# An encoder trunk on one core: weight splits on VectorE below chunk 60, delta-net matmuls interleaved by head and direction, and a shorter inverse square root

## The chip, the cores and the metric

The kernel runs on one core of a Trainium2 chip. A core has five engines that run side by side, each through its own instruction stream in order: TensorE (PE; its weight loads are listed as PEld), VectorE (DVE), ScalarE (ACT), GpSimd (POOL) and SyncE (SP), which here issues nearly all DMAs. Matmuls write to PSUM, of which VectorE and ScalarE read the results; the other operands lie in SBUF. The metric is the device time of one execution in microseconds; less is better.

## The reference, cut to what matters

Two residual layers on 512 tokens of width 1024, in float32. The part that the change touches is the bidirectional gated delta net; the rest is summarised in comments.

```python
for l in range(DEPTH):                       # DEPTH = 2
    h = rms_norm(x, attn_norm[l])
    # one projection h @ w_in: neighbourhood attention (4 heads), sliding-window
    # attention (8 query heads, 2 key heads, rotary), delta net, three merge gates
    y_na = neighborhood_attention_2d(rms_norm(qa), rms_norm(ka), va, na_rpb[l])
    y_swa = sliding_window_gqa(apply_rope(rms_norm(qs)), apply_rope(rms_norm(ks_)), vs, sink)
    y_gdn = gated_deltanet_bidir(qkv_c, z_c, beta_c, a_c, ...)
    merged = (g_na * (y_na @ w_branch_na[l]) + g_swa * (y_swa @ w_branch_swa[l])
              + g_gdn * (y_gdn @ w_branch_gdn[l]))
    x = x + merged @ w_out[l]
    h = rms_norm(x, ffn_norm[l])
    u = depthwise_conv_centred(h @ w_up[l], ffn_conv_w[l]) + ffn_conv_b[l]
    a, b = jnp.split(u, 2, axis=-1)
    x = x + (jax.nn.silu(a) * b) @ w_down[l]

def gated_delta_rule_chunked(q, k, v, beta, g):      # 4 heads, 8 chunks of 64, both directions
    g = jnp.cumsum(g, axis=-1)
    decay = jnp.exp(jnp.where(incl, g[..., :, None] - g[..., None, :], -jnp.inf))
    k_beta = k * beta[..., None]
    lower = jnp.where(strict, einsum('bhnid,bhnjd->bhnij', k_beta, k) * decay, 0.0)
    # (lower + I) is inverted: u, w = its products with beta v and beta k exp(g)
    qk = einsum('bhnid,bhnjd->bhnij', q, k) * decay
    def step(S, xs):                                 # over the 8 chunks
        v_new = u_c - w_c @ S
        o_c = q_c @ S + qk_c @ v_new
        S = S * d_c + k_c.T @ v_new
        return S, o_c

def rms_norm(x, g):                                  # an inverse square root per token (and head)
    return x * lax.rsqrt(jnp.mean(x * x, axis=-1, keepdims=True) + NORM_EPS) * g
```

## The kernel before, in words

Features lie on the partitions and the 512 tokens along the free axis. Every weight matrix is cut into 128 chunks per layer (`wall`, chunk numbers `CH_...`): 0 to 59 belong to the projections, gates, branch projections and the output projection of the attention half, 60 to 103 (`CH_UP`) to the up-projection, 104 to 127 (`CH_DN`) to the down-projection. A chunk has 8 blocks of 128x128 and is read in two halves of four blocks.

Each product of a dense layer keeps float32 accuracy with three matmuls (`mm3`, L150 to L152): high weight x high input, high x low, low x high. `load_w` prepares a half chunk: SyncE reads `raw`, ScalarE rounds it to the high part `hi` (L142), and GpSimd computes the low part `lo = raw - hi` (L144). `raw`, `hi` and `lo` have three buffers each; a new `hi` waits until TensorE has used up the one three halves earlier.

`rsq` (L166 to L173) gives inverse square roots on VectorE, on 4 to 32 columns: one integer operation for the start value, then three Newton steps of three operations each, ten instructions that depend on one another. It is called ten times in a layer: by `Stream.finish` for each of the two norms of the layer, by `knorm` for the keys (three times), for the query norms of both attentions, for the keys of the delta net, and twice at its output. `spread` multiplies its result by the constant `RSQ`, and transposes it back to the layout of the features (L193); `sums` makes the sums of squares with narrow matmuls (L179), copies them to a tile `sb` and transposes them (L183).

The delta net goes through `gdn_gates`, `gdn_project`, `gdn_cross`, `gdn_solve`, `gdn_mid`, `gdn_scan` and `gdn_out`. Two heads share 128 partitions (64 each), and so do the two directions in the solve and the scan. In `gdn_cross` a loop over the four heads makes the decays (L662, L670), and per half of four chunks four matmuls (L677) of 64 contraction rows, which start at partition 0 or 64 as the head is even or odd; each head's eight matmuls stand one behind another. VectorE multiplies the results with the decays (L681, L682), and the triangular blocks are copied to `Xg` and `Xo` by GpSimd and ScalarE (L687, L692). `gdn_solve` transposes these and inverts 32x32 blocks by substitution: 31 steps of a product (L713) and a subtraction (L715) on VectorE, each on all heads and chunks; then matmuls join the blocks (L749, L764). In `gdn_mid`, L794 and L812 are 64x64 matmuls that alternate between the two directions, which lie in the two halves of the partitions and of the array. `gdn_scan` runs over eight steps; in each, L832 (`w x S`) and L843 (`k x v_new`) are eight 64x64 matmuls, first the four heads of one direction and then those of the other, and VectorE adds the results (L835, L848).

The order of work: the code issues the steps in the order `sp np gg na gp sa gx gz gs gm gc go mn ms mg` (projections and attentions, the delta net's steps `g.`, then the three merges), and the framework's planner (`TileContext(..., schedule_with_timeline_sim=True)`) lays down the order of each engine's stream ahead of the run, from priorities and assumed durations; dense matmuls of the gates fill in between the attention's matmuls. On the chip each engine keeps to its stream and waits where an input is not there.

Of the kernel before, what the change touches and what calls it, by code (L numbers as in the profile page):

```python
# [35 lines left out]
CH_UP = 60  # L36
# [7 lines left out]
ENG = {}  # L44
FIRST = {"np": CH_NA, "sp": CH_SK, "gp": CH_GK}
RSQ_K = 2.0 ** -65.5626
RSQ = -RSQ_K / 8
CAPS = {n + i: c for n, c in (("nqs", 2), ("nkh", 2), ("y", 4), ("ma", 4), ("mg", 8), ("gt", 2), ("W", 2),
                              ("qd", 2), ("wn", 2), ("vs", 1), ("z", 1), ("act", 22)) for i in "01"}
CAPS |= {"ysh": 2, "ysl": 2, "kE": 4, "kT": 4, "Q": 4, "VN": 4, "SA": 4, "kq": 4, "dup": 5, "spr": 4, "xo": 4, "qs0": 4, "qs1": 4, "kdh0": 1, "kdh1": 1, "kdl0": 1, "kdl1": 1, "nkl0": 2, "nkl1": 2, "sv": 1, "hf": 8}  # L50
# [11 lines left out]
def encoder_kernel(ctx, tc, xT, wall, par, cst, nab, out, depth=2, dbg=None):  # L62
# [70 lines left out]
    def load_w(l, c, nk=8):  # L133
        if (l, c) in early:
            return early.pop((l, c))
        ws = []
        for o in range(0, nk, 4):
            n = min(4, nk - o)
            raw = wp.tile([128, 4, 128], F32, tag="raw", name=nm("wr"), bufs=NB["raw"])
            lastw[0] = nc.sync.dma_start(out=raw[:, :n], in_=wall[l, c, :, o * 128:(o + n) * 128].rearrange("p (k m) -> p k m", k=n))  # L140
            hi = wp.tile([128, 4, 128], F32R, tag="hi", name=nm("wh"), bufs=NB["hi"])
            S.activation(out=hi[:, :n], in_=raw[:, :n], func=AF.Copy)  # L142
            lo = wp.tile([128, 4, 128], F32R, tag="lo", name=nm("wl"), bufs=NB["lo"])
            G.tensor_tensor(lo[:, :n], raw[:, :n], hi.bitcast(F32)[:, :n], op=ALU.subtract)  # L144
            ws += [(hi[:, k], lo[:, k]) for k in range(n)]
        return ws

# [15 lines left out]
        V.tensor_tensor(lo, src, hi.bitcast(F32), op=ALU.subtract)  # L163


    def rsq(a, n):  # L166
        y, t = small(n, "rq"), small(n, "rt", 1)
        V.tensor_scalar(y.bitcast(I32), a.bitcast(I32), 1, 0x7FFFFFFF, op0=ALU.logical_shift_right, op1=ALU.bitwise_xor)
        for i in range(3):
            V.scalar_tensor_tensor(t, y, RSQ_K / 2 ** i, a, op0=ALU.mult, op1=ALU.mult)  # L170
            V.scalar_tensor_tensor(t, t, RSQ_K / 2 ** i, y, op0=ALU.mult, op1=ALU.mult)
            V.scalar_tensor_tensor(y, t, -3.0, y, op0=ALU.add, op1=ALU.mult)  # L172
        return y  # L173


    def sums(src, sel, tag, pb=None):
        pb = bank(tag)[:, 0:256] if pb is None else pb
        for b in range(4):
            T.matmul(pb[32 * b:32 * b + 32, 0:128], lhsT=sel, rhs=src[:, 128 * b:128 * b + 128], start=True, stop=True,  # L179
                     tile_position=(0, 32 * b))  # L180
        sb = tmp(name="sb")[:, 0:128]
        copy("sb", sb, pb[:, 0:128])
        T.transpose(pb[:, 128:256], sb, ident)  # L183
        return pb[:, 128:256].rearrange("p (b i) -> p b i", b=4)[:, :, 0:32:16]
# [51 lines left out]
    def n8(a):  # L236
        return a.rearrange("p (n i) -> p n i", n=8)
# [37 lines left out]
    for l in range(depth):  # L275
# [374 lines left out]
        def gdn_cross():  # L650
            line[0] = "g"
            nonlocal Q, Qu, Xo, Xg, Lt, Rt, kds, qdec

            Q, Qu = by2("Q")
            Xo, Xg, Lt = (big(F32, (128, 32, 32), name=n) for n in ("Xo", "Xg", "Lt"))
            kds = [[doubled(kq[j][i][:, :, 0, :]) for i in range(2)] for j in range(2)]
            qdec = pair(name="qd") + pair(name="qd")
            for hh in range(4):
                j, rr = hh // 2, slice(64 * (hh % 2), 64 * (hh % 2) + 64)
                pe, pr = decay_sums(hh, (msr, blk))  # L660
                eg = tmp(name="eg")
                S.activation(out=eg, in_=pr, func=AF.Exp)  # L662
                for d in range(2):
                    r = slice(64 * d, 64 * d + 64)
                    for i in range(2):
                        ns = slice(4 * i, 4 * i + 4)
                        V.tensor_tensor(n8(qdec[hh])[r, ns], n8(eg)[r, ns], kq[j][i][rr, :, 1, :], op=ALU.mult)  # L667
                T.matmul(pe, lhsT=idb, rhs=nmb.unsqueeze(1).to_broadcast([128, 8, 64]), start=False, stop=True)
                e = tmp(name="E")
                S.activation(out=e, in_=pe, func=AF.Exp)  # L670
                on("ebk", "V").tensor_tensor(n8(e), n8(e), bc(bk, hh, 0, 8), op=ALU.mult)
                xt = tmp(name="X")
                for n0 in (0, 4):
                    kd = kds[j][n0 // 4]
                    pk = bank("gd")
                    for n in range(4):
                        T.matmul(pk[:, 128 * n:128 * n + 128], lhsT=kd[rr, n].rearrange("p d i -> p (d i)"),  # L677
                                 rhs=kq[j][n0 // 4][rr, n].rearrange("p c i -> p (c i)"), start=True, stop=True)
                    pkv = pk.rearrange("p (n c i) -> p c n i", n=4, c=2)
                    en = n8(e)[:, n0:n0 + 4]  # L680
                    V.tensor_tensor(n8(xt)[:, n0:n0 + 4], pkv[:, 0], en, op=ALU.mult)  # L681
                    V.tensor_tensor(Qu[n0 // 4 * 2 + hh // 2][:, :, hh % 2], pkv[:, 1], en, op=ALU.mult)  # L682

                for q4 in range(4):
                    r = slice(32 * q4, 32 * q4 + 32)
                    o = 32 * (q4 % 2)
                    cpx = (S.activation if q4 % 2 else G.tensor_copy)(  # L687
                        out=Xg[r].rearrange("p i (h n) -> p h n i", h=4)[:, hh], in_=n8(xt)[r, :, o:o + 32], **({"func": AF.Copy} if q4 % 2 else {}))
                    if q4 == 2:
                        lastg[0] = cpx  # L690
                    if q4 in (0, 3):
                        S.activation(out=Xo[r, 8 * hh:8 * hh + 8], in_=n8(xt)[r, :, 32 - o:64 - o], func=AF.Copy)  # L692
            Rt = big(F32, (128, 32, 32), "Rt")

        def gdn_solve():
# [121 lines left out]
        def gdn_scan():  # L817
# [7 lines left out]
            for s in range(8):  # L825
                ns = (s, 7 - s)
                half = [slice(0, 64), slice(64, 128)]
                if s:
                    pv = bank("gd", (128, 4, 64))
                    for d, r in enumerate(half):  # L830
                        for hh in range(4):
                            T.matmul(pv[r, hh], lhsT=n8(wn[hh])[r, ns[d]], rhs=SA(ns[d])[r, hh], start=True, stop=True,  # L832
                                     tile_position=(64 * d, 64 * d))
                    for d, r in enumerate(half):
                        V.tensor_tensor(VN(ns[d])[r], pv[r], VN(ns[d])[r], op=ALU.add)  # L835
                if s < 7:
# [295 lines left out]
```

## Time and profile before

| | us |
|---|---|
| median of 3 runs | 1711.9 |
| lowest and highest | 1708.8, 1712.89 |
| profiled execution, its own time | 1711.75 |
| its span in the trace, first to last instruction | 1710.0 |
| TensorE, VectorE, GpSimd, ScalarE busy | 1656.6, 1008.1, 834.5, 739.1 |

The profile is of one execution. A busy time counts an engine from the start of an instruction to its end; matmuls overlap, so a TensorE that is busy all the time need not be at its peak. In layer 0 the attention half ends at about 502 us and the MLP at about 866; layer 1 follows. The rows below have times in us from the start of the span, unless they are marked ns.

### The profile page before, as it was taken

The page shows a single profiled execution, that of the slowest core. Times are in us where ns is not written, and L with a number is a line of the kernel's source. Part 1 is how long each engine was busy: PE and PEld are TensorE (multiplying, and loading weights), DVE is VectorE, ACT ScalarE, POOL GpSimd, SP SyncE. Part 2 cuts the span into 40 slices and gives each one's busy share as a digit, 9 for nine tenths or more (in the row PEclk, how much of TensorE's full clock was granted, in tenths as well). Part 3 has the DMA queues.
Part 4 walks back from the last instruction along what each step waited for, and adds up shares of the span by engine and source line. Part 5 has one row for each costly group of instructions (what it writes and reads, how often), then busy time and mean ns, then how long its engine had stood idle before and what let it go on. Part 6 is the DMA issues. An engine that isn't in the chain of part 4 may idle for free.

```text
span 1710.0 us, 25217 instructions
## 1 busy us (share of the span) xinstructions
PE 1656.6 (97%) x9196; PEld 1319.6 (77%) x9196; DVE 1008.1 (59%) x1809; ACT 739.1 (43%) x1436; POOL 834.5 (49%) x752
## 2 busy tenths in 40 slices
PE   7989999999999999999999998899999999999999
PEld 5766767777888888878886776777878888888887
DVE  5489996534547777741125898955255487777200
ACT  5445545423445444443334555554234354444321
POOL 4665442264544555544448554422644545555543
PEclk9989999999999999999999999999999999999999
DMA  5222211122452332234333221110324523222432
GB/s 205 74 64 76 70 62 45 38 69 73 132 190 87 99 99 96 96 115 132 114 104 94 67 72 56 56 44 26 99 91 138 178 87 99 93 93 92 136 121 70
DMA packets 91500, 160.46 MB, mean 94 GB/s; under 512 B 10352, under 2 KB 17136, under 8 KB 91376
## 3 DMA queue, kind: packets, MB, share of 16 engines
q1 hardware_dynamic: 91376, 158.85, 28.9%
q8 instruction: 72, 1.18, 0.3%
q14 instruction: 52, 0.43, 0.1%
HBM read 147.80 MB, written 8.39 MB: 91 GB/s over the span
## 4 chain that ended last, share of the span: by engine, by line
PE 79%; DVE 14%; issue 3%; ACT 2%; DMA 1%; POOL 0%; SPq 0%; DVEq 0%; ACTq 0%; POOLq 0%
PE mm L152 23%; PE mm L150 23%; PE mm L151 23%; DVE Rt L715 1%; DVE Tm L713 1%; PE at L535 1%; PE at L531 1%; DVE qd L667 1%; DVE lg L428 1%; DVE fix L172 1%; PE gd L843 1%; PE gd L832 1%; DVE fix L170 1%; PE gd L812 1%; PE at L509 1%
## 5 line engine op out<-in xcount | busy, mean ns | idle before, releaser
L144 POOL TENSOR_TENSOR wl<-wr,wh 128x512 fp32r<-128x512 f32 (+1 forms) x512 | 683.8, 1344 | 792.2 <-ACT wh L142 739.1
L150 PE MATMUL mm<-hh,wh 128*128 128x512 f32 x1408 | 560.2, 398 | 15.3 <-ACT wh L142 13.1
L152 PE MATMUL mm<-hh,wl 128*128 128x512 f32 x1408 | 559.3, 399 | 1.8 <-POOL wl L144 1.7
L151 PE MATMUL mm<-hl,wh 128*128 128x512 f32 x1408 | 556.0, 395 | 0.1
L142 ACT ACTIVATE wh<-wr 128x512 fp32r<-128x512 f32 (+1 forms) x512 | 312.4, 617 | 354.7 <-PE mm L151 213.0
L150 PEld LDWEIGHTS mm<-hh,wh 128*128 128x128 f32 x1408 | 268.0, 190 | 74.2 <-ACT wh L142 15.9
L152 PEld LDWEIGHTS mm<-hh,wl 128*128 128x128 f32 x1408 | 267.7, 190 | 65.1 <-POOL wl L144 6.2
L151 PEld LDWEIGHTS mm<-hl,wh 128*128 128x128 f32 x1408 | 267.7, 190 | 58.3 <-issue 1.9
L234 DVE SCALAR_TENSOR_TENSOR cv<-up,fix,cv 128x511 f32<-128x511 f32 x88 | 142.0, 1613 | 2.8
L233 DVE SCALAR_TENSOR_TENSOR cv<-up,fix,cv 128x511 f32<-128x511 f32 x88 | 85.9, 977 | 88.5 <-ACT cv L232 88.5
L152 PE MATMUL mm<-act,wl 128*128 128x512 f32 x352 | 137.2, 390 | 0.6 <-POOL wl L144 0.6
L150 PE MATMUL mm<-act,wh 128*128 128x512 f32 x352 | 137.1, 389 | 0.3 <-ACT wh L142 0.3
L151 PE MATMUL mm<-act,wh 128*128 128x512 f32 x352 | 137.0, 389 | 0.0
L971 DVE TENSOR_TENSOR xo<-xo,mm 128x512 f32<-128x512 f32 x16 | 11.0, 687 | 192.3 <-PE mm L152 192.3
L232 ACT ACTIVATE cv<-up,fix 128x512 f32<-128x512 f32 x88 | 70.8, 809 | 34.7 <-DVE up L280 34.7
L162 ACT ACTIVATE act<-cv 128x512 fp32r<-128x512 f32 x44 | 27.8, 632 | 126.0 <-DVE cv L954 126.0
L152 PEld LDWEIGHTS mm<-act,wl 128*128 128x128 f32 x352 | 66.1, 188 | 15.3 <-POOL wl L144 1.3
L150 PEld LDWEIGHTS mm<-act,wh 128*128 128x128 f32 x352 | 66.1, 188 | 14.2 <-ACT wh L142 0.7
L151 PEld LDWEIGHTS mm<-act,wh 128*128 128x128 f32 x352 | 66.1, 188 | 13.7
L953 ACT ACTIVATE cv<-cv 128x512 f32<-128x512 f32 x44 | 27.8, 633 | 86.2 <-DVE cv L234 86.2
L280 DVE TENSOR_TENSOR up<-mm,rstd 128x512 f32<-128x512 f32 x88 | 59.5, 680 | 8.2 <-ACT rstd L228 8.2
L900 ACT ACTIVATE gt<-gt 128x512 f32<-128x512 f32 x48 | 30.2, 630 | 66.4 <-DVE gt L280 66.3
(285 smaller groups left out, 2228.5 us busy)
## 6 DMA issues: line engine op xcount, KB each, us to landing
wr<-in_wall_dram SPq DMA_DIRECT2D x496, 256.0 KB, 2.8
xs<-xo SPq DMA_DIRECT2D x24, 256.0 KB, 2.9
xo<-xs SPq DMA_DIRECT2D x24, 256.0 KB, 3.7
xo<-in_xT_dram SPq DMA_DIRECT2D x16, 256.0 KB, 4.9
sw<-raw SPq DMA_DIRECT2D x40, 64.0 KB, 2.0
wr<-in_wall_dram SPq DMA_DIRECT2D x16, 128.0 KB, 3.3
out_dram<-xo SPq DMA_DIRECT2D x8, 256.0 KB, 2.1
nab<-in_nab_dram SPq DMA_DIRECT2D x8, 248.0 KB, 2.8
```

The lines of the kernel that those rows point to most:

```text
L142: S.activation(out=hi[:, :n], in_=raw[:, :n], func=AF.Copy)
L144: G.tensor_tensor(lo[:, :n], raw[:, :n], hi.bitcast(F32)[:, :n], op=ALU.subtract)
L150: T.matmul(acc, lhsT=wh, rhs=rh, start=start, stop=False)
L151: T.matmul(acc, lhsT=wh, rhs=rl, start=False, stop=False)
L152: T.matmul(acc, lhsT=wl, rhs=rh, start=False, stop=stop)
L162: S.activation(out=hi, in_=src, func=AF.Copy)
L232: S.activation(out=dst, in_=src, func=AF.Identity, scale=w[:, 1:2], bias=bias)
L233: V.scalar_tensor_tensor(dst[:, 1:L], src[:, 0:L - 1], w[:, 0:1], dst[:, 1:L], op0=ALU.mult, op1=ALU.add)
L234: V.scalar_tensor_tensor(dst[:, 0:L - 1], src[:, 1:L], w[:, 2:3], dst[:, 0:L - 1], op0=ALU.mult, op1=ALU.add)
L280: V.tensor_tensor(dst, acc, rstd, op=ALU.mult)
L900: S.activation(out=gt[q], in_=gt[q], func=AF.Tanh, scale=0.5)
L953: S.activation(out=cv[0], in_=cv[0], func=AF.Silu)
```

## The change

Five edits. In `load_w` the low part of chunks below `CH_UP` (60) is computed by VectorE instead of GpSimd; the MLP's chunks keep GpSimd. `rsq` takes one third-order step (four operations) and one Newton step (three) after its start value, eight instructions instead of ten, and `RSQ` takes up the changed constant. The tile `sb` in `sums` has 128 columns instead of 512. `gdn_cross` works through heads in pairs: first the decays of both, then the matmuls L677 of the two heads in turn (an even head on partitions 0 to 63, an odd one on 64 to 127, each into its own PSUM bank), then the multiplications and the copies of both. In `gdn_scan` the matmuls L832 and L843 run over heads outside and directions inside, so that the two directions alternate.

```diff
-RSQ = -RSQ_K / 8
+RSQ = -RSQ_K * 3 / 16
...
             lo = wp.tile([128, 4, 128], F32R, tag="lo", name=nm("wl"), bufs=NB["lo"])
-            G.tensor_tensor(lo[:, :n], raw[:, :n], hi.bitcast(F32)[:, :n], op=ALU.subtract)
+            (G if c >= CH_UP else V).tensor_tensor(lo[:, :n], raw[:, :n], hi.bitcast(F32)[:, :n], op=ALU.subtract)
...
-        for i in range(3):
-            V.scalar_tensor_tensor(t, y, RSQ_K / 2 ** i, a, op0=ALU.mult, op1=ALU.mult)
-            V.scalar_tensor_tensor(t, t, RSQ_K / 2 ** i, y, op0=ALU.mult, op1=ALU.mult)
-            V.scalar_tensor_tensor(y, t, -3.0, y, op0=ALU.add, op1=ALU.mult)
+        V.scalar_tensor_tensor(t, y, RSQ_K, a, op0=ALU.mult, op1=ALU.mult)
+        V.scalar_tensor_tensor(t, t, RSQ_K, y, op0=ALU.mult, op1=ALU.mult)
+        V.scalar_tensor_tensor(t, t, -10.0 / 3.0, t, op0=ALU.add, op1=ALU.mult)
+        V.scalar_tensor_tensor(y, t, 5.0, y, op0=ALU.add, op1=ALU.mult)
+        V.scalar_tensor_tensor(t, y, 0.375 * RSQ_K, a, op0=ALU.mult, op1=ALU.mult)
+        V.scalar_tensor_tensor(t, t, 0.375 * RSQ_K, y, op0=ALU.mult, op1=ALU.mult)
+        V.scalar_tensor_tensor(y, t, -3.0, y, op0=ALU.add, op1=ALU.mult)
...
-        sb = tmp(name="sb")[:, 0:128]
+        sb = tmp(shape=(128, 128), name="sb")
...
-            for hh in range(4):
-                j, rr = hh // 2, slice(64 * (hh % 2), 64 * (hh % 2) + 64)
-                pe, pr = decay_sums(hh, (msr, blk))
...
+            for j in range(2):
+                es, xts = [], []
+                for e in range(2):
+                    hh, rr = 2 * j + e, slice(64 * e, 64 * e + 64)
+                    pe, pr = decay_sums(hh, (msr, blk))
...
                 for n0 in (0, 4):
                     kd = kds[j][n0 // 4]
-                    pk = bank("gd")
+                    pks = [bank("gd") for _ in range(2)]
                     for n in range(4):
-                        T.matmul(pk[:, 128 * n:128 * n + 128], lhsT=kd[rr, n].rearrange("p d i -> p (d i)"),
-                                 rhs=kq[j][n0 // 4][rr, n].rearrange("p c i -> p (c i)"), start=True, stop=True)
+                        for e in range(2):
+                            rr = slice(64 * e, 64 * e + 64)
+                            T.matmul(pks[e][:, 128 * n:128 * n + 128], lhsT=kd[rr, n].rearrange("p d i -> p (d i)"),
+                                     rhs=kq[j][n0 // 4][rr, n].rearrange("p c i -> p (c i)"), start=True, stop=True)
...
-                    for d, r in enumerate(half):
-                        for hh in range(4):
+                    for hh in range(4):
+                        for d, r in enumerate(half):
                             T.matmul(pv[r, hh], lhsT=n8(wn[hh])[r, ns[d]], rhs=SA(ns[d])[r, hh], start=True, stop=True,
                                      tile_position=(64 * d, 64 * d))
...
                             G.tensor_tensor(sd[r], SA(ns[d])[r], hn(dec[:, 64:96])[r, :, ns[d]].unsqueeze(2).to_broadcast([64, 4, 64]), op=ALU.mult)
-                        for hh in range(4):
+                    for hh in range(4):
+                        for d, r in enumerate(half):
                             T.matmul(pd[r, hh], lhsT=kT(ns[d], hh)[r], rhs=VN(ns[d])[r, hh], start=True, stop=True,
                                      tile_position=(64 * d, 64 * d))
```

## Rows read from the trace of the kernel before

**Rows 1.** The page: span, busy time by engine, granted clock in 40 slices.
```profile
span 1710.0 us, 25217 instructions
...
PE 1656.6 (97%) x9196; PEld 1319.6 (77%) x9196; DVE 1008.1 (59%) x1809; ACT 739.1 (43%) x1436; POOL 834.5 (49%) x752
...
PEclk9989999999999999999999999999999999999999
```

**Rows 2.** Windows, all engines: stretch, its length, busy us (xcount) by engine, PEclk, DMA.
```profile
27.00:120.00 93.00, 84.64 (x452) 65.04 (x451) 60.07 (x133) 41.40 (x81) 58.22 (x45) 0.94 0.23 72
120.00:200.00 80.00, 75.97 (x420) 56.31 (x418) 70.55 (x147) 48.14 (x115) 47.07 (x79) 0.98 0.23 69
200.00:260.00 60.00, 52.93 (x286) 40.04 (x287) 57.70 (x130) 28.44 (x67) 25.15 (x28) 0.96 0.23 70
260.00:400.00 140.00, 139.88 (x1303) 108.23 (x1300) 65.21 (x180) 58.24 (x139) 52.90 (x49) 0.98 0.17 54
400.00:502.00 102.00, 101.47 (x512) 83.25 (x511) 56.83 (x91) 43.36 (x72) 47.63 (x36) 1.00 0.42 138
502.00:866.00 364.00, 363.11 (x1607) 299.20 (x1606) 196.23 (x224) 150.64 (x247) 181.99 (x137) 1.00 0.33 106
...
890.00:960.00 70.00, 62.91 (x330) 47.47 (x328) 43.66 (x89) 30.20 (x59) 47.06 (x35) 0.90 0.27 84
960.00:1040.00 80.00, 77.72 (x430) 59.67 (x429) 71.92 (x162) 50.04 (x112) 47.89 (x46) 1.00 0.22 67
1040.00:1105.00 65.00, 55.61 (x281) 42.37 (x279) 61.78 (x144) 30.02 (x75) 28.33 (x62) 0.97 0.18 61
```

**Rows 3.** Windows of line L144 alone (the split on GpSimd), the same columns.
```profile
27.00:120.00 93.00, 32.75 (x25) 0.94 0.23 72
120.00:200.00 80.00, 22.05 (x16) 0.98 0.23 69
200.00:260.00 60.00, 18.57 (x14) 0.96 0.23 70
...
960.00:1040.00 80.00, 23.69 (x17) 1.00 0.22 67
1040.00:1105.00 65.00, 20.77 (x16) 0.97 0.18 61
```

**Rows 4.** Timeline of the substitution: start us, duration us, instruction.
```profile
231.19 1.29 POOL L144 TENSOR_TENSOR wl<-wr,wh 128x512 fp32r<-128x512 f32 x1 [6.23 <-ACT wh L142]
231.26 1.48 DVE L713 TENSOR_TENSOR Tm<-Lt,Rt 128x231 f32<-128x231 f32 x1
...
234.32 0.39 DVE L713 TENSOR_TENSOR Tm<-Lt,Rt 128x220 f32<-128x220 f32 x1
```

**Rows 5.** Source line L172, an `rsq` step: duration ns min/median/max, first and last start.
```profile
L172 DVE SCALAR_TENSOR_TENSOR fix<-fix x60: 153/169/1331, 33.6 to 1361.2; 128x8 f32<-128x8 f32 x30, 128x4 f32<-128x4 f32 x12, 128x32 f32<-128x32 f32 x12, 128x16 f32<-128x16 f32 x6
```

**Rows 6.** Source line L954, 128x512 from two SBUF tiles, the same columns.
```profile
L954 DVE TENSOR_TENSOR cv<-cv,cv x44: 674/692/694, 530.7 to 1594.3; 128x512 f32<-128x512 f32 x44
```

**Rows 7.** Pieces of the chain that ended last: start us, duration us, what.
```profile
286.79 1.54 PE gd L794 x46
290.21 0.96 PE gd L794 x28
...
329.94 0.89 PE gd L832 x16
...
1010.47 1.09 PE gd L677 x8
```

**Rows 8.** Waits of TensorE from 27 to 120: us in total, times, longest.
```profile
PE at L193 <- DVE rb L190: 6.6, 2, 5.9
```

**Rows 9.** Waits of GpSimd from 200 to 260, the same columns.
```profile
POOL wl L144 <- ACT wh L142: 27.8, 8, 6.2
```

More of the change, by code (lines that the diff above doesn't have):

```diff
@@ L657, in gdn_cross @@
             qdec = pair(name="qd") + pair(name="qd")
-            for hh in range(4):
-                j, rr = hh // 2, slice(64 * (hh % 2), 64 * (hh % 2) + 64)
-                pe, pr = decay_sums(hh, (msr, blk))
[L661 to L672, printed above, removed]
+            for j in range(2):
[3 more added lines that the diff above has]
+                    pe, pr = decay_sums(hh, (msr, blk))
+                    eg = tmp(name="eg")
+                    S.activation(out=eg, in_=pr, func=AF.Exp)
+                    for d in range(2):
+                        r = slice(64 * d, 64 * d + 64)
+                        for i in range(2):
+                            ns = slice(4 * i, 4 * i + 4)
+                            V.tensor_tensor(n8(qdec[hh])[r, ns], n8(eg)[r, ns], kq[j][i][rr, :, 1, :], op=ALU.mult)
+                    T.matmul(pe, lhsT=idb, rhs=nmb.unsqueeze(1).to_broadcast([128, 8, 64]), start=False, stop=True)
+                    ex = tmp(name="E")
+                    S.activation(out=ex, in_=pe, func=AF.Exp)
+                    on("ebk", "V").tensor_tensor(n8(ex), n8(ex), bc(bk, hh, 0, 8), op=ALU.mult)
+                    es.append(ex)
+                    xts.append(tmp(name="X"))
@@ L673, in gdn_cross @@
                 for n0 in (0, 4):
                     kd = kds[j][n0 // 4]
-                    pk = bank("gd")
+                    pks = [bank("gd") for _ in range(2)]
                     for n in range(4):
-                        T.matmul(pk[:, 128 * n:128 * n + 128], lhsT=kd[rr, n].rearrange("p d i -> p (d i)"),
-                                 rhs=kq[j][n0 // 4][rr, n].rearrange("p c i -> p (c i)"), start=True, stop=True)
-                    pkv = pk.rearrange("p (n c i) -> p c n i", n=4, c=2)
@@ L680, in gdn_cross @@
[L680 to L692, printed above, removed]
+                        for e in range(2):
+                            rr = slice(64 * e, 64 * e + 64)
+                            T.matmul(pks[e][:, 128 * n:128 * n + 128], lhsT=kd[rr, n].rearrange("p d i -> p (d i)"),
+                                     rhs=kq[j][n0 // 4][rr, n].rearrange("p c i -> p (c i)"), start=True, stop=True)
@@ new lines, in gdn_cross @@
+                    for e in range(2):
+                        pkv = pks[e].rearrange("p (n c i) -> p c n i", n=4, c=2)
+                        en = n8(es[e])[:, n0:n0 + 4]
+                        V.tensor_tensor(n8(xts[e])[:, n0:n0 + 4], pkv[:, 0], en, op=ALU.mult)
+                        V.tensor_tensor(Qu[n0 // 4 * 2 + j][:, :, e], pkv[:, 1], en, op=ALU.mult)
+                for e in range(2):
+                    hh = 2 * j + e
+                    for q4 in range(4):
+                        r = slice(32 * q4, 32 * q4 + 32)
+                        o = 32 * (q4 % 2)
+                        cpx = (S.activation if q4 % 2 else G.tensor_copy)(
+                            out=Xg[r].rearrange("p i (h n) -> p h n i", h=4)[:, hh], in_=n8(xts[e])[r, :, o:o + 32], **({"func": AF.Copy} if q4 % 2 else {}))
+                        if q4 == 2:
+                            lastg[0] = cpx
+                        if q4 in (0, 3):
+                            S.activation(out=Xo[r, 8 * hh:8 * hh + 8], in_=n8(xts[e])[r, :, 32 - o:64 - o], func=AF.Copy)
```

## The prediction

> **What bounds the kernel now.** The page comes first: over the whole span TensorE is busy 97%, VectorE 59%, GpSimd 49% [rows 1]. A share like that hides stages, so the table by stretches is read next [rows 2]. In the stretch 502 to 866, the up- and down-projections of layer 0, TensorE is busy 363.11 of 364 us over 1607 matmuls: 0.2265 us from one 128x512 matmul to the next, with no wait that the table shows. From 260 to 502 it is the same (139.88 of 140, 101.47 of 102). There only less TensorE work can save time. From 27 to 260 TensorE is idle 8.4, 4.0 and 7.1 us, 19.5 us in all; in layer 1, from 890 to 1105, 7.1, 2.3 and 9.4, 18.8 us. [...]
>
> In the same stretches VectorE is the fullest of the other engines: 70.55 of 80 us and 57.70 of 60 us in layer 0, 71.92 of 80 and 61.78 of 65 in layer 1 [rows 2]. From 120 to 260 (960 to 1105) VectorE sets the end: attention softmax, delta-net decays and the 31-step substitution are all its work, and TensorE fills in.
>
> Much of this VectorE time is not work. At 231.26 the substitution's product (L713) takes 1.48 us because a weight split on GpSimd (L144) began 0.07 us before; one step later the same operation takes 0.39 us [rows 4]. An `rsq` step (L172) on at most 32 columns has a median of 169 ns and a maximum of 1331 ns [rows 5]. Each GpSimd split can so stop one VectorE instruction for about its own 1.29 us.
>
> **Part 1: the splits move to VectorE.** For chunks below 60 (all of attention and the output projection) GpSimd loses its splits: 25, 16 and 14 in the three stretches of layer 0, 17 and 16 in the two full ones of layer 1 [rows 3]. On VectorE a 128x512 operation with two inputs in SBUF has a median of 0.692 us (L954) [rows 6]; that is the price of one split. What a removed split gives back is bounded by nothing (it met only idle time or PSUM-fed work) and by 1.48 - 0.39 = 1.09 us [rows 4]. VectorE is busy nine tenths in the full stretches and most of its operations there read two SBUF tiles, so I take 0.75 us, nearer the upper end. Per split that is 0.75 - 0.69 = -0.06 us; over the 63 splits of the full stretches (30 + 33), -4 us. But GpSimd keeps other work there, 47.07 - 22.05 = 25.0 us of 80, and 25.15 - 18.57 = 6.6 us of 60 [rows 2, 3], and a split on VectorE can be stopped by it as an `rsq` step is: 16 x 31% + 14 x 11% = 6.5 splits per layer, half a GpSimd instruction (0.65 us) each, 4.2 us per layer, if these met at random. The planner spreads such work, and GpSimd's own operations will run earlier without splits ahead of them, so I take half, +4 us. **Term: 0 us**, bounds +43 (63 x 0.69) and -25 (63 x (1.09 - 0.69)).
>
> [...]
>
> From 260 on VectorE has room (65.21 of 140 us, 56.83 of 102 [rows 2]), and TensorE's weights are ready three half chunks ahead (three buffers each of raw, high and low), some 8 us at 12 x 0.2265 us each: the splits there cost nothing. Without that cover they would cost 0.69 us each.
>
> **Part 2: the order on VectorE.** GpSimd spent much of its time waiting for the high part: 27.8 us in 8 waits from 200 to 260 alone, the longest 6.2 [rows 9]. ScalarE writes that part when TensorE gives a buffer back. On VectorE the same wait would hold everything queued behind it: a substitution step, a softmax scale, and through them TensorE's transposes. The order of each engine is fixed by a planner that assumes durations; where it places the split after the high part is due, nothing waits. Bounds: nothing, and 27.8 us per layer if VectorE inherits that stretch's waits whole. VectorE waits hardly at all there now, which says that the planner's order is near enough. **Term: +4 us** (2 per layer).
>
> **Part 3: `rsq`.** Ten instructions become eight; nothing is issued elsewhere. Of its 20 calls (10 per layer) those in the merge and before the up-projection lie behind TensorE's filled queue and are worth nothing; without that cover, two steps of 0.17 us. Two calls per layer stand in the full stretch: 2 x 2 x 2 steps x 0.169 = 1.4 us, up to 10 us if all were stopped for 1.3 us each. **Term: -2 us.**
>
> **Part 4: the chains from 27 to 120 and 890 to 960.** TensorE's idle time here is 8.4 and 7.1 us [rows 2]; 6.6 of the first are two waits of the transposes at L193 for the tile that follows an `rsq` [rows 8]. Ten steps of `rsq` cost 1.7 us undisturbed and up to 13 us when each meets GpSimd [rows 5]. GpSimd is busy 58.22 us of the 93, 32.75 of it splits [rows 2, 3], so 56% of the meetings go, and two of ten steps. What is late next is the rotary exchange (a DMA, unchanged) and GpSimd's own residuals, which now start without splits ahead of them. Bounds: nothing, -15.5 us. **Term: -8 us**, about half.
>
> **Part 5: the scan's order (L832, L843).** A run of 16 instructions (each of the 8 float32 matmuls shows as two) takes 0.89 us. The runs of L794, which already alternate between the two halves of the array, take 1.54 us for 46 and 0.96 for 28 [rows 7]: 0.0322 us each, so 0.57 us for 16. Per run 0.32 us; 7 + 7 runs in each of 2 layers make 28, 8.9 us. TensorE is full there, so it counts; the fixed entry into a run may be more than the line through two longer runs says, so I take **-8 us**, bounds 0 (if the scan waits for VectorE instead) and -8.9.
>
> **Part 6: the paired delta-net products (L677).** Eight instructions take 1.09 us [rows 7]; 2 layers x 4 heads x 2 halves are 16 such runs, 17.4 us. Alternating heads may overlap them as far as L794 does (nearly half, -8) or not at all. They lie where VectorE sets the end, so TensorE time freed there is mostly idle: **-2 us**, bounds 0 and -8. The VectorE and ScalarE operations of the pair are the same in number; the smaller `sb` tile costs nothing.
>
> [...]
>
> **Sum.** 0 + 4 - 2 - 8 - 8 - 2 = -16 us, against the profiled execution's 1711.75 us (span 1710.0; median of the runs 1711.9, the same within 0.01%): **1696 us**, -0.9%.
>
> **Rivals.**
> *The full stretch opens up* (chance 0.17). If splits give back 1.0 us each, the full stretches lose 63 x 0.31 = 20 us more; TensorE's idle time there is 4.0 + 7.1 + 2.3 + 9.4 = 22.8, which caps it. For it: the pair at 231. Against it: GpSimd's remaining work. With two thirds of the cap, -15: 1681.
> *The swap gives nothing* (0.16). The splits on VectorE cost what they free, remaining GpSimd work stops them (part 1, +8 at full price), and part 4's idle time moves to the next link. Then the scan's -8 is offset: 1712, or no change; the same if the alternating order does not overlap.
> *VectorE waits for the high part* (0.22). Place: the substitution, 200 to 260 and 1040 to 1105. Price: more than half of the 27.8 us that GpSimd waits there now, 16 per layer, 32 us in place of my 4: 1696 + 28 = 1724, slower. It decides from about 12 us per layer on. For it: the wait is real and VectorE is at 96% there. Against: a split that the planner puts later does not wait.
>
> **Numbers.** Forecast 0.45. Its own range is 1688 to 1705. Eight in ten lie between 1677 and 1720: the low end is the first rival, the high end most of the third. Faster by more than 0.3% (5.1 us, about what a measurement of this kernel can tell from no change) 0.63; within it 0.15; slower 0.22.
>
> **What would show it.** Right: no L144 on GpSimd before 460 us and from 870 to 1300; `rsq` steps near 170 ns in most cases; runs of L832 and L843 at 0.57 to 0.65 us; L713 and L715 seldom above 1 us; TensorE idle from 27 to 120 near 4 us. Wrong: VectorE waits on ScalarE's L142 ahead of L144 in the substitution, TensorE's idle time from 120 to 260 above 15 us, or a solve (the first L713 to L749) longer than 60 us; the prediction fails most likely through the planner's new order, which no row of before shows.

## The result, and the profile after

The changed kernel takes 1684.8 us (median of 4 runs, 1684.2 to 1686.2), the kernel before 1712.4 in the same comparison (4 runs, 1708.8 to 1715.8): ratio 0.984, interval 0.9819 to 0.9862, 27.6 us less. The forecast was 1696 and the range 1677 to 1720: the sign and the range held, and the gain is 11 us larger than the likeliest case, below that case's own lower end of 1688.

The page of the changed kernel: span, busy time by engine, and the shares of the chain that ended last.

```profile
span 1682.4 us, 25082 instructions
...
PE 1641.7 (98%) x9196; PEld 1313.7 (78%) x9196; DVE 1054.1 (63%) x2009; ACT 739.0 (44%) x1436; POOL 528.5 (31%) x512
...
PE 87%; DVE 7%; issue 2%; ACT 1%; POOL 1%; DMA 1%; SPq 0%; POOLq 0%; DVEq 0%; ACTq 0%
```

Against [rows 1], GpSimd is busy 306 us less and VectorE only 46 us more, although VectorE took over 240 splits. TensorE has the same 9196 matmuls. VectorE holds 7% of the chain; on the page of before it held 14%.

Line numbers from `rsq` on moved: an `rsq` step is now at L176, the paired products (L677) at L687, the copies of Xg at L700, the substitution (L713, L715) at L726 and L728, the solve's product L749 at L762, the scan (L832, L843) at L845 and L857, the transposes of [rows 8] at L197.

Windows of the changed kernel over all engines, columns as in [rows 2]; the last two are layer 1, counted from 849, where its first weights reach TensorE:

```profile
27.00:120.00 93.00, 92.36 (x500) 71.13 (x498) 64.07 (x158) 48.32 (x96) 26.75 (x19) 1.00 0.29 89
120.00:200.00 80.00, 74.81 (x406) 56.81 (x406) 70.60 (x180) 43.53 (x103) 27.15 (x63) 0.94 0.22 66
200.00:260.00 60.00, 56.65 (x371) 43.48 (x370) 48.58 (x119) 30.96 (x68) 6.84 (x14) 0.90 0.23 72
849.00:942.00 93.00, 89.06 (x466) 69.53 (x465) 56.99 (x117) 40.47 (x79) 26.37 (x19) 0.94 0.32 97
942.00:1087.00 145.00, 140.72 (x752) 109.40 (x750) 131.89 (x340) 83.58 (x190) 31.86 (x75) 0.99 0.23 70
```

From 27 to 120 TensorE's idle time went from 8.4 us [rows 2] to 0.6, and its granted clock from 0.94 to 1.00. From 120 to 260 it has 776 matmuls where before had 706, but the granted clock fell, from 0.98 and 0.96 to 0.94 and 0.90. In layer 1 less of the idle time went. The same stretches of the kernel before, counted from 862, where its layer 1 starts, have 7.1 us idle each, the changed kernel 3.9 and 4.3:

```profile
862.00:955.00 93.00, 85.91 (x444) 65.80 (x443) 50.10 (x96) 40.16 (x77) 59.16 (x45) 0.93 0.30 94
955.00:1100.00 145.00, 137.86 (x728) 106.01 (x727) 130.46 (x311) 79.08 (x182) 72.74 (x101) 0.99 0.20 63
```

Where the time came from is read from work done, not from idle time. L150 is one of the three matmuls of each dense step, so 3 x 0.2265 = 0.68 us of TensorE for each. Windows of L150 alone (busy us and xcount of the matmul, of the weight load, then clock, DMA share, GB/s), first the kernel before, then the changed one:

```profile
27.00:120.00 93.00, 38.65 (x97) 18.47 (x97) 0.94 0.23 72
120.00:260.00 140.00, 47.47 (x116) 22.29 (x116) 0.97 0.23 70
260.00:502.00 242.00, 99.41 (x253) 47.80 (x253) 0.99 0.27 89
862.00:955.00 93.00, 39.66 (x98) 19.11 (x98) 0.93 0.30 94
955.00:1100.00 145.00, 52.96 (x133) 25.16 (x133) 0.99 0.20 63
1100.00:1349.00 249.00, 100.37 (x255) 48.22 (x256) 0.99 0.28 89
```

```profile
27.00:120.00 93.00, 44.42 (x112) 20.88 (x112) 1.00 0.29 89
120.00:260.00 140.00, 48.13 (x116) 22.69 (x116) 0.92 0.22 68
260.00:502.00 242.00, 98.67 (x252) 47.28 (x253) 0.98 0.28 90
849.00:942.00 93.00, 41.77 (x106) 20.21 (x105) 0.94 0.32 97
942.00:1087.00 145.00, 58.32 (x145) 27.36 (x144) 0.99 0.23 70
1087.00:1336.00 249.00, 100.04 (x256) 48.11 (x257) 0.99 0.30 95
```

Layer 0: 15 more dense steps from 27 to 120 (15 x 0.68 = 10.2 us), none in the full stretch, one fewer behind it. Layer 1: 8 more in its first 93 us (5.4 us), 12 more in its full stretch (8.2), one more behind it. These 35 steps are 24 of the 27.6 us. Layer 1's first dense matmul starts at 849.3 instead of 861.8, so layer 0 gave 12.5 us and layer 1 the other 15.1.

### The profile page after: what moved, and what is told of

Read it like the earlier page. It is cut to its first block, busy times and chain, and to the rows that moved or that the text cites. A ratio compares the mean times of both kernels' runs of the same rounds, so it can differ in the third digit from the quotient of the medians.

```text
span 1682.4 us, 25082 instructions
## 1 busy us (share of the span) xinstructions
PE 1641.7 (98%) x9196; PEld 1313.7 (78%) x9196; DVE 1054.1 (63%) x2009; ACT 739.0 (44%) x1436; POOL 528.5 (31%) x512
## 4 chain that ended last, share of the span: by engine, by line
PE 87%; DVE 7%; issue 2%; ACT 1%; POOL 1%; DMA 1%; SPq 0%; POOLq 0%; DVEq 0%; ACTq 0%
PE mm L152 26%; PE mm L150 26%; PE mm L151 25%; PE at L539 1%; PE at L535 1%; DVE wl L144 1%; PE at L513 1%; PE gd L825 1%; PE gd L807 1%; PE at L514 1%; PE gd L762 0%; DVE spr L529 0%; PE at L442 0%; PE gd L845 0%; PE gd L857 0%
## 5 line engine op out<-in xcount | busy, mean ns | idle before, releaser
L150 PE MATMUL mm<-hh,wh 128*128 128x512 f32 x1408 | 558.1, 397 | 8.2 <-ACT wh L142 6.8
L144 POOL TENSOR_TENSOR wl<-wr,wh 128x512 fp32r<-128x512 f32 (+1 forms) x272 | 364.0, 1350 | 535.8 <-ACT wh L142 528.3
L150 PEld LDWEIGHTS mm<-hh,wh 128*128 128x128 f32 x1408 | 266.9, 190 | 66.9 <-ACT wh L142 8.2
L144 DVE TENSOR_TENSOR wl<-wr,wh 128x512 fp32r<-128x512 f32 x240 | 174.4, 730 | 76.0 <-ACT wh L142 68.9
L150 PE MATMUL mm<-act,wh 128*128 128x512 f32 x352 | 137.1, 389 | 0.1
L985 DVE TENSOR_TENSOR xo<-xo,mm 128x512 f32<-128x512 f32 x16 | 11.0, 687 | 181.1 <-PE mm L152 181.1
L150 PEld LDWEIGHTS mm<-act,wh 128*128 128x128 f32 x352 | 66.1, 188 | 14.1 <-ACT wh L142 0.5
L854 POOL TENSOR_TENSOR sd<-SA,fix 64x256 f32<-64x256 f32 x24 | 15.5, 646 | 162.7 <-DVE SA L864 119.8
```

Of the source, the lines that this page charges most:

```text
L144: (G if c >= CH_UP else V).tensor_tensor(lo[:, :n], raw[:, :n], hi.bitcast(F32)[:, :n], op=ALU.subtract)
L150: T.matmul(acc, lhsT=wh, rhs=rh, start=start, stop=False)
```

## The experiments

Ratios are to the kernel before, timed beside each run on the same chip, with their intervals; gains in us are worked out from them.

**One part alone, on the kernel before.** Four kernels, each with one part of the diff.

`only_lo`, VectorE's low parts:

```diff
-            G.tensor_tensor(lo[:, :n], raw[:, :n], hi.bitcast(F32)[:, :n], op=ALU.subtract)
+            (G if c >= CH_UP else V).tensor_tensor(lo[:, :n], raw[:, :n], hi.bitcast(F32)[:, :n], op=ALU.subtract)
```

> The kernel before with one edit: the low parts of chunks below 60 on VectorE. Theory 1 (the edits add up, each at its own price, as the prediction has it): the freed chains from 27 to 120 and 890 to 960 and an even swap elsewhere, -4 to -10 us. Theory 2 (GpSimd's splits stopping VectorE were nearly the whole loss): -20 to -27 us, with the inverse-root steps near 170 ns and the substitution's operations near 340 ns. Theory 3 (any edit makes the planner lay all streams anew, and the new order is what is measured): any value, unlike what the traces of the single operations say.

Measured: 1691.2 us, 0.9882 [0.9867, 0.9897], 20 us faster.

`only_rsq`, eight instructions for an inverse root in place of ten (the diff's hunk at L166 with its constant RSQ):

> The kernel before with one edit: the inverse roots in eight instructions instead of ten. GpSimd's splits stay where they were. Theory 1: -2 to -4 us. Theory 2: the steps that remain are stopped by GpSimd as before (up to 1.3 us each), two fewer of ten: -2 to -5 us. Theory 3: a change of more than 5 us in either direction.

Measured: 1717.6 us, 1.004 [1.0028, 1.0052], 7 us slower.

`only_cross`, the paired delta-net products (the diff's hunk at L655 with `sb`):

> The kernel before with one edit: the delta net's products taken through heads in pairs. Theory 1: -2 us, and the products' runs take about half of 1.09 us per eight instructions. Rival: the planner issues most of a head's four matmuls in one piece all the same, because only three PSUM banks of this kind exist and one is still held by the second head's decays; then the pitch stays at 0.112 us and the time within 3 us. Theory 3: more than 5 us in either direction.

Measured: 1713.8 us, 1.0023 [1.0014, 1.0031], 4 us slower.

`only_scan`, the alternating order in the scan:

```diff
-                    for d, r in enumerate(half):
-                        for hh in range(4):
+                    for hh in range(4):
+                        for d, r in enumerate(half):
```

> The kernel before with one edit: in the scan, heads outside and directions inside. Theory 1: runs of 16 instructions take 0.62 us instead of 0.89, 28 runs, and as TensorE is full there, -7 us. Rival: the run is shorter but starts only when VectorE's result is there, or is broken by waits for the second direction's result, so that the two lines' time stays at about 26 us and the whole within 3 us.

Measured: 1704.3 us, 0.9965 [0.9953, 0.9978], 6 us faster.

What follows: the low parts carry the change, the scan adds its own, and the other two are not gains by themselves. The four add up to -20 + 7 + 4 - 6 = -15 us, and together they give -27.6: they are not additive. Where the low parts act is seen in the start of layer 1: 849.2 us in `only_lo`, 849.3 in the changed kernel, 861.8 before. So in layer 0 they give the whole gain, and in layer 1 7.3 of the 15.1 us (840.9 us from there to the end of the span, against 848.2 before and 833.1 in the changed kernel).

**One part taken out of the changed kernel.**

`no_lo`, the reverse of the edit of `only_lo`:

> The changed kernel with the low parts of all chunks on GpSimd again; the other edits stay. If the edits add up from what they gave alone on the kernel before (inverse root +7, pairs +4, scan -6 us) it is about 1716 us. If the shorter inverse root and the pairs pay only once GpSimd no longer stops VectorE, it is near the kernel before, 1705 to 1720, and the changed kernel's -27 us is then -20 for the move and -7 for the others in its presence. If the move were worth less inside the changed kernel than alone, it is under 1705.

Measured: 1714.8 us, 1.0025 [1.0012, 1.0038]. Without the low parts the other three together cost 4 us, and the low parts are worth 0.0185 of the time before, 32 us, beside them.

`no_cross`, the four heads one after the other again:

> The changed kernel with the delta net's products taken head by head again. In the changed kernel only two of eight product pairs really alternate, so by its own price the edit is worth 1 to 2 us: 1685 to 1687. If the pairs matter through the order that the planner makes (the substitution starts some 20 us earlier in the changed kernel), more: 1690 or above. Below 1683 the pairs cost time.

Measured: 1687.6 us, 0.9867 [0.9852, 0.9883]: pairing is worth 3 to 5 us here, and the intervals overlap.

**Is it GpSimd's operations that stop VectorE, or the way of the low part?** `dummy` leaves the splits on VectorE and gives GpSimd, for each of the 240, an operation of the same size whose result nothing reads:

```diff
+            if c < CH_UP:
+                du = wp.tile([128, 4, 128], F32, tag="du", name=nm("wd"), bufs=2)
+                G.tensor_tensor(du[:, :n], hi.bitcast(F32)[:, :n], hi.bitcast(F32)[:, :n], op=ALU.subtract)
```

> The changed kernel, in which GpSimd besides subtracts the high part from itself for every half chunk below 60, into a tile that nothing reads: the same number, size and place of GpSimd instructions as in the kernel before, and no result that anything waits for. Theory 2 (a GpSimd instruction that reads SBUF stops VectorE): the gain of the move is lost and more, since VectorE now has both the splits and the stops: 1705 to 1730, substitution operations again with maxima near 1.4 us. Rival (the gain came from the shorter way of the low part to TensorE, 0.7 instead of 1.3 us, and from GpSimd's queue): 1685 to 1690.

Measured: 1733.6 us, 1.0134 [1.012, 1.0148]: some 49 us above the changed kernel. The same VectorE split, on the page of the changed kernel and then of `dummy` (busy us and mean ns of one, then idle time before it):

```profile
L144 DVE TENSOR_TENSOR wl<-wr,wh 128x512 fp32r<-128x512 f32 x240 | 174.4, 730 | 76.0 <-ACT wh L142 68.9
```

```profile
L144 DVE TENSOR_TENSOR wl<-wr,wh 128x512 fp32r<-128x512 f32 x240 | 224.8, 940 | 55.7 <-ACT wh L142 53.3
```

730 ns became 940 ns, with the same operands. The added operation also holds a buffer of the high part: ScalarE waited for it 8 times, 12.0 us in all, a side effect that is far smaller than the 49 us. It reads SBUF and writes it; by which of its properties it costs VectorE this time was not tried. Source line of the substitution's subtraction (L715 before, L728 after, L731 in `dummy`; duration ns min/median/max), one fence for each:

```profile
L715 DVE TENSOR_TENSOR Rt<-Rt,Tm x62: 191/373/1492, 199.7 to 1094.2; 128x31 f32<-128x31 f32 x4, 128x60 f32<-128x60 f32 x4, 128x87 f32<-128x87 f32 x4, 128x112 f32<-128x112 f32 x4
```

```profile
L728 DVE TENSOR_TENSOR Rt<-Rt,Tm x62: 182/358/425, 183.3 to 1077.5; 128x31 f32<-128x31 f32 x4, 128x60 f32<-128x60 f32 x4, 128x87 f32<-128x87 f32 x4, 128x112 f32<-128x112 f32 x4
```

```profile
L731 DVE TENSOR_TENSOR Rt<-Rt,Tm x62: 176/378/1261, 203.1 to 1123.5; 128x31 f32<-128x31 f32 x4, 128x60 f32<-128x60 f32 x4, 128x87 f32<-128x87 f32 x4, 128x112 f32<-128x112 f32 x4
```

The median hardly differs; what comes and goes is the tail, 1492, 425 and 1261 ns. The chains ahead of the full stretch show it too: windows of `dummy`'s first dense matmul (its L153), and TensorE's wait for the tile after an `rsq` from 27 to 120 (us in total, times, longest; its L200 is the L193 of [rows 8]):

```profile
27.00:120.00 93.00, 39.39 (x100) 18.79 (x100) 0.96 0.25 77
```

```profile
PE at L200 <- DVE rb L197: 5.1, 1, 5.1
```

100 dense steps where the changed kernel has 112 and the kernel before 97, and 5.1 us of wait where [rows 8] has 6.6.

**How far must VectorE take the splits?** `v20` and `v30` stop earlier: `CH_UP` is replaced by `CH_MG[0]` (c < 20, 80 splits) and by `CH_MG[1]` (c < 30, 120 splits).

```diff
-            (G if c >= CH_UP else V).tensor_tensor(lo[:, :n], raw[:, :n], hi.bitcast(F32)[:, :n], op=ALU.subtract)
+            (G if c >= CH_MG[0] else V).tensor_tensor(lo[:, :n], raw[:, :n], hi.bitcast(F32)[:, :n], op=ALU.subtract)
```

> The changed kernel with VectorE's low parts only for chunks below 20 (projections, used up to about 200 us into a layer); the gates, branch and output projections (20 to 59) have theirs on GpSimd again. If the gain sits in the chains of the projections, before the substitution, most of it stays: 1685 to 1692. If it sits in the substitution, whose filling matmuls use chunks 20 to 29, those operations are stopped again (maxima near 1.4 us) and it is 1697 to 1708.

> The changed kernel with VectorE's low parts for chunks below 30 only (projections and the first gate); the chunks that run beside and after the scan have theirs on GpSimd. If the moved splits are free from 260 us of a layer on (TensorE is full there either way), within 3 us of the changed kernel: 1682 to 1688. If they hold up VectorE's part of the scan, faster: 1675 to 1681. If GpSimd's splits stop VectorE in the scan as well, slower: 1690 or above.

Measured: `v20` 1698.5 us, 0.9921 [0.9905, 0.9938]; `v30` 1691.3 us, 0.9888 [0.9873, 0.9902]. In `v20` the splits are back on GpSimd from 142 us on. Its windows of L150, and its source line L728:

```profile
27.00:120.00 93.00, 44.29 (x112) 21.04 (x112) 1.00 0.28 88
120.00:260.00 140.00, 44.49 (x107) 20.85 (x106) 0.90 0.21 65
```

```profile
L728 DVE TENSOR_TENSOR Rt<-Rt,Tm x62: 175/368/1510, 183.5 to 1077.5; 128x31 f32<-128x31 f32 x4, 128x60 f32<-128x60 f32 x4, 128x87 f32<-128x87 f32 x4, 128x112 f32<-128x112 f32 x4
```

The first window keeps the whole gain (112 dense steps), the second loses 9 against the changed kernel (6 us), and the substitution's long stops are back (1510 ns). `v30`, whose last VectorE split of layer 0 starts at 231 us, has 112 and 117, as many as the changed kernel, and layer 1 starts at 849.1 us, as there. What `v30` loses against the changed kernel (6.4 us; the intervals do not overlap) lies in layer 1 behind 1087: 247 dense steps to 1336 instead of 256, 6.1 us, at a granted clock of 0.97 instead of 0.99. So the splits from 231 us of a layer on were worth nothing in layer 0 and some 6 us in layer 1, which another layout of the streams may also give (see the length of `rsq`). That GpSimd's splits stopped VectorE in the scan, as the expectation would have it, is not shown: layer 0 has the same scan and lost nothing.

The page's busy times of these kernels (VectorE is DVE) make a ledger of the exchange; each split's own price is its row's mean:

```profile
PE 1652.0 (96%) x9196; PEld 1310.5 (77%) x9196; DVE 999.1 (58%) x1769; ACT 736.6 (43%) x1436; POOL 837.8 (49%) x752
```

```profile
PE 1654.0 (97%) x9196; PEld 1316.0 (78%) x9196; DVE 1008.3 (59%) x1849; ACT 737.7 (43%) x1436; POOL 730.0 (43%) x672
...
L144 DVE TENSOR_TENSOR wl<-wr,wh 128x512 fp32r<-128x512 f32 x80 | 58.8, 740 | 53.1 <-ACT wh L142 45.9
```

```profile
PE 1649.6 (98%) x9196; PEld 1317.5 (78%) x9196; DVE 999.0 (59%) x1889; ACT 738.7 (44%) x1436; POOL 676.4 (40%) x632
...
L144 DVE TENSOR_TENSOR wl<-wr,wh 128x512 fp32r<-128x512 f32 x120 | 86.7, 726 | 55.9 <-ACT wh L142 49.1
```

```profile
PE 1657.8 (96%) x9196; PEld 1317.9 (76%) x9196; DVE 1175.8 (68%) x2009; ACT 738.9 (43%) x1436; POOL 827.6 (48%) x752
```

VectorE without its splits: 999.1 us in `no_lo`; 1008.3 - 58.8 = 949.5 in `v20`; 999.0 - 86.7 = 912.3 in `v30`; 1054.1 - 174.4 = 879.7 in the changed kernel; the other instructions are 1769 in each. So 80 splits gave back 49.6 us of other VectorE work (0.62 each), the first 120 gave 86.8 (0.72 each), and the 120 behind them 32.6 (0.27 each). The second 40 alone, which in layer 0 run from 142 to 231 us, gave back 949.5 - 912.3 = 37.2, 0.93 each, and cost (86.7 - 58.8) / 40 = 0.70. VectorE's busy time differs by some 5 us between kernels with the same number of instructions and all splits on GpSimd (993.7 in `only_rsq`, 999.1 in `no_lo`), so the 0.93 is good to about 0.13. `dummy` closes the ledger: 240 GpSimd operations, 1175.8 - 1054.1 = 121.7 us more on VectorE, 0.51 each, what all 240 splits gave back on leaving GpSimd (119.4).

**The length of `rsq`.** `rsq10` and `rsq11` add two and three instructions to each of the 20 calls of the changed kernel; `rsq11` has the line below once more. The values stay the same.

```diff
+        V.tensor_scalar(t, t, 1.0, None, op0=ALU.mult)
+        V.tensor_scalar(t, t, 1.0, None, op0=ALU.mult)
```

> The changed kernel with two more instructions in each inverse root (multiplications by 1), ten as before. By price: 2 steps of 0.17 us for the calls on the path, 1 to 4 us: 1686 to 1689. If only the new order of the planner mattered, any value from 1680 to 1695.

> The changed kernel with three more instructions in each inverse root, eleven in all, where ten gave 1678.5 us and eight 1684.8. If longer inverse roots were better for a reason of their own (VectorE's splits come at a better moment), it stays at 1675 to 1680 or falls further. If the planner's new order sets the difference and has nothing to do with the count, any value from 1675 to 1695. By the price of the instructions alone (3 x 0.17 us for the calls on the path) it would be 1686 to 1690.

Measured: 8, 10 and 11 instructions take 1684.8, 1678.5 (0.9802 [0.9789, 0.9815]) and 1698.1 us (0.9919 [0.9899, 0.9938]). More work on VectorE was first faster, then slower: the count is not the cause. The planner lays out all engines anew for each edit, and that layout is what remains as a cause; no run holds it fixed. `rsq10` is the fastest kernel of all here. One thing in which the layouts differ shows in windows of 10 us, TensorE alone (busy us and xcount, granted clock, DMA share, GB/s), of the changed kernel and then of `rsq10`:

```profile
170.00:180.00 10.00, 6.67 (x37) 0.82 0.16 50
180.00:190.00 10.00, 8.14 (x28) 0.67 0.16 52
240.00:250.00 10.00, 6.75 (x70) 0.90 0.02 6
250.00:260.00 10.00, 10.00 (x105) 0.50 0.24 76
```

```profile
170.00:180.00 10.00, 8.51 (x51) 1.00 0.16 46
180.00:190.00 10.00, 8.15 (x33) 0.83 0.29 78
240.00:250.00 10.00, 9.79 (x111) 1.00 0.03 9
250.00:260.00 10.00, 10.00 (x130) 0.66 0.27 82
```

From 250 to 260 the changed kernel's TensorE is busy all 10 us at a granted clock of 0.50, after it sat idle 3.25 us of the 10 before; `rsq10` sat idle 0.21 us and was granted 0.66. In all other windows of 10 us from 120 to 260 both were granted 1.00, so the missing clock is (0.18 + 0.33 + 0.10 + 0.50) x 10 = 11.1 us against (0.17 + 0.34) x 10 = 5.1 in `rsq10`; the times differ by 6.4. That agrees for this pair and for no more: `rsq11` is missing 5.1 us there too (0.70, 0.96 and 0.83 in the windows from 180, 190 and 250) and is 20 us slower than `rsq10`. From 27 to 502 it has 473 dense steps, the changed kernel 480 and `rsq10` 488.

**Alternating all the paired products.** In the changed kernel two of the eight groups of 16 instructions at L687 alternate as the source says, and the planner put most of the others one head after the other. `forced` chains them in the order of the source:

```diff
+                            with (tc.issue_after(lastp.ins) if lastp else nullcontext()):
+                                lastp = T.matmul(pks[e][:, 128 * n:128 * n + 128], ...)
```

> The changed kernel with the paired products' issue order fixed (each product behind the one before it), so that the two heads alternate in all eight groups and not in two. By the price of the alternating groups in the changed kernel's trace (0.056 us per instruction against 0.112) TensorE needs 5 us less for them: 1680 if that counts, since TensorE is nearly full in the changed kernel. If VectorE sets the end there, no change: 1683 to 1687. If the fixed order makes one head's products wait for the other's bank, slower.

Measured: 1685.7 us, 0.986 [0.9841, 0.9879], no change. Pieces of the chain (start us, duration us) of the changed kernel and then of `forced`:

```profile
142.87 1.10 PE gd L687 x16
...
995.66 1.08 PE gd L687 x8
```

```profile
150.72 1.09 PE gd L689 x14
```

Alternating, 16 products take 1.10 us and 14 take 1.09; in a row, 8 take 1.08. The overlap is there, and it does not show in the time.

## Why the prediction was right, and where it was too small

**Part 1, the splits (term 0).** The price of a split was right: 0.69 us taken, 0.73 measured. What it gives back was taken as 0.75 us in the full stretch and is not the same everywhere: 0.62 for the first 80 splits, 0.93 for the next 40, which lie in that stretch. So VectorE gained more there than the term has, near the 1.0 of the first rival. On TensorE it came out otherwise in each layer. In layer 0's full stretch the count of dense steps is the same, 116 and 116. In layer 1's it is not: 133 to 145, 8.2 us, inside the bound of -25 but taken as zero. TensorE sat idle 145 - 140.72 = 4.3 us there against 7.1 in the same stretch before, which is 2.9 of the 8.2. In layer 0 the stretch did more as well, 70 more matmuls, all small, but the clock of 140 us fell from 0.97 to 0.92, and from 260 to 400 TensorE was idle 4.7 us where [rows 2] has 0.1; no dense step came of it by 502. That GpSimd's remaining work would go on stopping VectorE did not show in the full stretches: the longest substitution step is 426 ns, the longest split 0.83 us in layer 0 and 0.92 in layer 1. It did show ahead of them, where splits took up to 1.77 us.

`dummy`'s added operations cost 0.51 us of VectorE each; the remaining ones show no such cost in the full stretches (no split above 0.92 us), so the term's +4 for them is not seen there. VectorE operations that read PSUM were not stopped on the trace of before: L835 takes 416 to 429 ns in all 28, 16 of them beside a GpSimd operation of over 1 us, where L715, from two SBUF tiles, takes up to 1492.

**Part 2 (term +4).** VectorE's waits from 120 to 260 of the changed kernel (us in total, times, longest):

```profile
DVE wl L144 <- ACT wh L142: 3.2, 3, 1.6
```

3.2 us in layer 0, near the 2 per layer taken, and far from the 12 at which the third rival decides. That rival did not happen. VectorE does wait for the high part, 68.9 us over the span (the page's L144 row above), but hardly where it sets the end: 3.2 us from 120 to 260 and 0.4 from 942 to 1087. The term came true by another way, which the prediction had not seen: the split waits behind VectorE's other work, and TensorE for the split. In layer 0 a high part was written by 175.5 us and its split began at 181.1. TensorE's waits for the low part, from 120 to 260 and from 942 to 1087:

```profile
PE mm L152 <- DVE wl L144: 2.7, 1, 2.7
...
PE mm L152 <- DVE wl L144: 3.4, 1, 3.4
```

On the page of before, the same product lost 1.7 us to splits on GpSimd, so 4.4 us were added, near the +4.

**Part 3 (term -2).** Not shown. The steps run at 169 ns undisturbed, as expected; source line L176 of the changed kernel (duration ns min/median/max):

```profile
L176 DVE SCALAR_TENSOR_TENSOR fix<-fix x20: 156/168/194, 32.2 to 1333.0; 128x8 f32<-128x8 f32 x10, 128x4 f32<-128x4 f32 x4, 128x32 f32<-128x32 f32 x4, 128x16 f32<-128x16 f32 x2
```

But alone the edit costs 7 us, two more instructions per call took 6 us off and one more put 20 on; a term of 2 us cannot be read under that.

**Part 4, the chains ahead of the full stretch (term -8).** This is the term that was mis-sized. The mechanism is as put: the wait of [rows 8] is the row that shrank, from 6.6 us to

```profile
PE at L197 <- DVE rb L194: 0.6, 1, 0.6
```

It measured 10.2 us in layer 0 and 5.4 in layer 1, 15.6 together, twice the term. The step that failed is taking half of the idle time because 56% of the meetings go, and it failed in layer 0: from 27 to 120 no Newton step of `rsq` was longer than 0.30 us, the integer step ahead of them was stopped once (1.17 us), and 0.6 us of 8.4 stayed idle. The 7.8 us freed hold 7.8 / 0.2265 = 34 of the 45 added dense matmuls; the other eleven, 2.5 us, go with the granted clock, 0.94 to 1.00, of which the bound of 15.5 held nothing. In layer 1 the half was about right for the idle time: 7.1 us before, 3.9 after, and the wait of [rows 8] is still 2.3 us there. GpSimd's remaining work still stops `rsq` steps on the way to it, as pieces of the chain that ended last show (start us, duration us; while the second ran, a GpSimd operation of 1.34 us at L489 did too):

```profile
923.94 1.07 DVE fix L169
925.27 1.17 DVE fix L171
```

That layer 1 has 5.4 us of added dense steps from 3.2 us of idle time is not explained. `dummy` shows the cause in layer 0: with GpSimd's operations back, and the splits still on VectorE, 12 of the 15 dense steps are lost again.

**Part 5, the scan (term -8).** Right in kind, and 1 to 2 us too large: `only_scan` gave -6 (interval 4 to 8), and both lines in both layers took 27.9 us before and 21.0 there, 6.9 less. Windows of its first line in layer 0, L832 before, in `only_scan` and in `only_lo`, then L845 after:

```profile
0.00:502.00 502.00, 6.73 (x112) 5.78 (x112) 0.98 0.28 91
```

```profile
0.00:502.00 502.00, 4.85 (x112) 3.89 (x112) 0.99 0.30 92
```

```profile
0.00:502.00 502.00, 7.83 (x112) 6.77 (x112) 0.97 0.30 94
```

```profile
0.00:502.00 502.00, 5.93 (x112) 4.65 (x112) 0.97 0.29 94
```

6.73 to 4.85 us for seven runs is 0.96 to 0.69 us each, not 0.57; the fixed entry into a run that the term mentioned would do that, but no row separates it. With VectorE's low parts the same products in the old order take 7.83, in the new 5.93: the saving holds in the rows, on a higher level. It does not show in layer 0's time: from 260 to 502 the dense steps are 260 in `only_scan`, but 252 in `only_lo` and 252 in the changed kernel, and layer 1 starts at the same time in both.

**Part 6 (term -2).** Small, as taken. The reason given, that TensorE time freed there is idle, fits and was not tried by itself. The overlap shows, 1.10 us for 16 alternating against 1.08 for 8 in a row, but `forced`, with all groups alternating, is not faster.

**The sum.** With parts 4 and 1 as measured, -15.6 and -8.2 in place of -8 and 0, the working's -16 becomes -31.8; the measured -27.6 lies 4 us from it, less than a new layout moves. That nearness is in part luck: the dense steps of parts 4 and 1 are 23.8 us of the gain and leave 3.8 for all the rest, the scan's -8 among it. By its number the result lies between the forecast and the first rival (1681); by mechanism it is the forecast with layer 1's part of that rival. The sign named as wrong, a solve longer than 60 us, did occur, without the loss that it was to announce. In layer 0 it took 64 us (L726 at 182.7 to L762 at 246.3; before, L713 at 199.5 to L749 at 259.0), but started 17 us earlier and ended 13 earlier. In layer 1 it took 69 us instead of 60 and ended 243.8 us behind the layer's first dense matmul, before 243.2.

**Open.** Why one layout of the planner is up to 20 us better than another: the clock agrees in one pair and not in the next, and no run changed it alone. And 8.2 - 2.9 = 5.3 us of layer 1's full stretch, which its idle time does not explain.

## What to carry to other kernels

Where a GpSimd stream of SBUF work runs beside a full VectorE, count what it takes from VectorE before counting what it saves: here moving 0.73 us operations over gave back as much VectorE time as they cost for the first half of a layer's splits (0.72 us each), more where VectorE was fullest (0.93), and the chains of short operations ahead of TensorE lost most of their stops (idle time 8.4 to 0.6 us in layer 0, 7.1 to 3.9 in layer 1). For such a gain, put the whole idle time that the stops cause, with the clock that comes back with it, inside the range: one layer got nearly all of it, the other half. Where a planner lays out all engines, an edit of one instruction per call moved the time by up to 20 us of 1700, so an effect of a few us has to be read in its own rows and not in the total.

## What was not expected of the hardware

The exchange is the same from both sides: 240 GpSimd operations of some 1.3 us each gave back 0.50 us of VectorE each on leaving, and took 0.51 on coming back in another form. The median of the substitution's subtraction hardly moved (358 to 378 ns); the longest durations did (425 against 1492 ns).

Idle time of TensorE can be followed by a lower clock, but does not tell it: in the changed kernel 3.25 us idle between 240 and 250 were followed by ten busy microseconds granted 0.50, and in `rsq10` 0.21 us idle were followed by 0.66.
